# Gate blocks: the one-hot array of second indices stored token by token instead of four tokens interleaved

## The chip, the cores and the metric

One core of one Trainium2 chip. The metric is device microseconds of one execution of the whole program, taken as the median of several runs. Lower is better.

## What is computed

Two transformer-like blocks on 512 tokens of width 1024, all in float32 at the interface. What matters here is the second half of the first block, a mixture over 16384 tiny experts (128 x 128 keys), cut from the reference:

```python
sc = jnp.einsum('phcd,hcnd->phcn', q, sub_keys)            # 8 heads, 2 halves, 128 keys
top_s, top_i = lax.top_k(sc, 16)                           # best 16 keys of each half
cand_s = top_s[:, :, 0, :, None] + top_s[:, :, 1, None, :] # 16 x 16 pairs
best_s, best_pos = lax.top_k(cand_s, 16)
idx = take_along_axis(cand_i, best_pos)                    # i * 128 + j of 16 experts per head
g = softmax(best_s)
act = gelu(einsum('phkd,pd->phk', expert_u[idx], xb))
out = einsum('phk,phkd->pd', g * act, expert_v[idx])
```

So each token selects 128 experts (8 heads times 16), each with an index pair (i, j) and a weight g.

## The kernel before

The kernel runs the first block (`first`), the experts (`peer`) and the second block (`second`) one after the other. Float32 products are made of three passes: `split` writes a high part (ScalarE, L93) and a low part (L94) of an operand, and `mm3` issues three matmuls per 128-row piece (L116, L118, L119).

In `peer`, the first 384 tokens (three tiles of 128) don't gather their experts. They multiply by all 16384 of them, in 128 steps of 128 experts: a **u-step** (`u_step`) makes the activations of 128 experts for 384 tokens, with 24 matmuls of 384 columns into the tile `act`; a later v-step multiplies these by the gates and by `expert_v` (tile `po`). The gates are a table in DRAM, `gdram`, with g at [j, i] of each token and zeros elsewhere. The fourth tile of tokens gathers rows of its experts with indirect DMAs (`gsteps`, tile `row`), with the dot products on VectorE (L656).

**The gate table** is built in `gates(tt)` for one tile of 128 tokens, in 16 **blocks** of 8 tokens. After a transpose, partition = one of the token's 128 choices, column = token. Per block, VectorE writes three float16 arrays of 128 x 1024: `oj` is 1 where column j equals the choice's j (L807, `is_equal`), `oi` the same for i (L808), `oa` = `oi` times the high half of g (L809), and `oi` is overwritten with `oi` times the low half (L810). All three are laid out [2 groups][128 columns][4 tokens]: the four tokens of a group are interleaved, so the 128 columns of one token lie 4 elements (8 bytes) apart. Then `products` issues, per token, two matmuls that accumulate into one 128 x 128 piece of the tile `pg`: weights `oj` against moving `oa` (L820), and weights `oj` against moving `oi` (L822). Each matmul loads its weights anew. That makes 16 matmuls with 16 weight loads a block and 768 of each in the 48 blocks. ScalarE copies `pg` to the tile `stage` (L824, twice a block); every second block one DMA takes `stage` to `gdram`.

The arrays of a block come from a pool with 4 buffers (`ohp`), so VectorE can be four blocks ahead of TensorE. `pg` has 3 buffers, `stage` 2.

**What sets the order.** `chain()` is a generator that emits top-k work (`choose`), then the gates of tile order[1], the last `choose`, and the gates of order[2] and order[3]. Each `yield` reports an estimated VectorE cost. A planner adds these costs up in `now`, and TensorE's in `pe`: 4.2 a u-step and 1.8 a block's products. Whenever `pe` is behind `now`, it emits a u-step (which adds 1.25 to `now` if its low parts are made on VectorE, as in `gates`) and, after two of three of them, one step of the fourth tile's gathers (1.3). The products of a block are put off by 9 units of `now`. It holds back the last 10 of the 88 u-steps of this stage until the chain has ended. The order in which each engine then runs its work is made from this emission order by a scheduler at build time, which can move instructions past each other where data and buffers allow. After the stage, the angles of the second block are computed in a `stage` buffer (`tr`) and stored (`csd`), and the v-steps begin with a load of `gdram` (tile `G`).

The lines that are touched: L695 to L698 (the column numbers 0 to 127: `io32` as int32, `iota4` as float16, each number four times), L806 and L807 (`oj`), L820 and L822 (the weight operand), and L831 (the estimated VectorE cost of a block).

Of the kernel before, what the change touches and what calls it, by code (L numbers as in the profile page):

```python
# [7 lines left out]
F32 = mybir.dt.float32  # L8
F32R = mybir.dt.float32r
F16 = mybir.dt.float16  # L10
I32 = mybir.dt.int32
U32 = mybir.dt.uint32
AF = mybir.ActivationFunctionType
ALU = mybir.AluOpType
# [4 lines left out]
P = 128  # L19
# [50 lines left out]
class K:  # L70
# [516 lines left out]
    def peer(self):  # L587
# [3 lines left out]
        with ExitStack() as ctx:  # L591
# [99 lines left out]
            for r in range(16):  # L691
                nc.gpsimd.memset(stc[:, r], float(STARTS[r]))
                nc.gpsimd.memset(wtc[:, r], float(STARTS[r] - STARTS[r - 1]) if r else 0.0)
                nc.gpsimd.memset(btc[:, r], float(r))
            io32 = tkp.tile([P, P], I32, name="io32")  # L695
            nc.gpsimd.iota(io32, pattern=[[1, P]], base=0, channel_multiplier=0)
            iota4 = tkp.tile([P, P, 4], F16, name="iota4")
            nc.vector.tensor_copy(iota4, io32[:, :, None].to_broadcast([P, P, 4]))  # L698
            consts = (stc, wtc, btc)

# [39 lines left out]
            with ExitStack() as pctx:  # L740
                rp.append(self.pool("ring", 1, None, rctx, "right"))
                stgp = self.pool("stg", 2, ctx=pctx)
                ohp = self.pool("oh", 4, ctx=pctx)
                pps = self.pool("pps", 2, PSUM, pctx)
                pgs = self.pool("pgs", 3, PSUM, pctx)
                pacts.append(self.pool("pact2", 1, PSUM, pctx))


                now, pe = [0.0], [U_LATE]
                queue = []  # L750

                def later(fn, cost=0.0):
                    queue.append((now[0] + LAG, fn, cost))

                def drain(all=False):
                    while queue and (all or queue[0][0] <= now[0]):
                        _, fn, cost = queue.pop(0)
                        first = fn()
                        if cost:
                            self.after(first, u_mark[0])  # L760
                            pe[0] += cost

                def choose(n):
                    tt = order[n]
                    res = gres if tt == NT else {n: tkp.tile([P, P], F32, name="tr" + n, bufs=2) for n in "ijg"}

                    def load():
                        if n + 1 < len(order):
                            sc[0] = score_tile()
                            nc.sync.dma_start(sc[0].rearrange("p a b -> p (a b)"), scd[order[n + 1]])  # L770

                    yield from self.topk(sc[0], tkp, consts, res, load)
                    if tt == NT:
                        gf = tkp.tile([P, P], F32, name="gf")
                        nc.vector.scalar_tensor_tensor(gf, gres["i"], 128.0, gres["j"], op0=ALU.mult, op1=ALU.add)
                        nc.vector.tensor_copy(gidx, gf)
                        self.early = 0
                    else:
                        def turn():
                            pt = turned[tt] = pps.tile([P, 3, P], F32, name="pt", tag="pps")  # L780
                            return [nc.tensor.transpose(pt[:, n], res[x], self.ident) for n, x in enumerate("ijg")][0]

                        later(turn, 0.4)

                turned = {}

                def gates(tt):

                    while tt not in turned:
                        yield 0.5, False  # L790
                    pt = turned[tt]
                    it = tkp.tile([P, 2, P], F16, name="it", bufs=2)
                    nc.vector.tensor_copy(it, pt[:, :2])
                    gs = tkp.tile([P, P], F32, name="gs", bufs=2)
                    nc.vector.tensor_scalar(gs, pt[:, 2], 2048.0, None, op0=ALU.mult)
                    gt = tkp.tile([P, 2, P], F16, name="gt", bufs=2)
                    nc.vector.tensor_copy(gt[:, 0], gs)
                    nc.vector.tensor_tensor(gt[:, 1], gs, gt[:, 0], op=ALU.subtract)
                    yield 1.0, False
                    stage = {}  # L800
                    for n in range(P // 8):
                        def bc(x):
                            return x[:, n * 8:n * 8 + 8].rearrange("p (g t) -> p g t", t=4)[:, :, None, :] \
                                .to_broadcast([P, 2, P, 4])
                        io = iota4[:, None].to_broadcast([P, 2, P, 4])
                        oj, oi, oa = [ohp.tile([P, 2, P, 4], F16, name=x) for x in ("oj", "oi", "oa")]  # L806
                        nc.vector.tensor_tensor(oj, io, bc(it[:, 1]), op=ALU.is_equal)  # L807
                        nc.vector.tensor_tensor(oi, io, bc(it[:, 0]), op=ALU.is_equal)  # L808
                        nc.vector.tensor_tensor(oa, oi, bc(gt[:, 0]), op=ALU.mult)  # L809
                        nc.vector.tensor_tensor(oi, oi, bc(gt[:, 1]), op=ALU.mult)  # L810

                        def products(n=n, oj=oj, oi=oi, oa=oa):
                            b, half = divmod(n, 2)
                            if half == 0:
                                stage[b] = stgp.tile([P, P, TB], F32, name="stage", tag="stage")
                            first = None
                            for q in range(2):
                                ps = pgs.tile([P, 4, P], F32, name="pg")
                                for t in range(4):
                                    ins = nc.tensor.matmul(ps[:, t], oj[:, q, :, t], oa[:, q, :, t], start=True, stop=False)  # L820
                                    first = first or ins
                                    nc.tensor.matmul(ps[:, t], oj[:, q, :, t], oi[:, q, :, t], start=False, stop=True)  # L822
                                c = half * 8 + q * 4
                                nc.scalar.activation(stage[b][:, :, c:c + 4].rearrange("p i t -> p t i"), ps,  # L824
                                                     AF.Copy, scale=1.0 / 2048.0)
                            if half:
                                nc.sync.dma_start(gdram[tt * (P // TB) + b], stage[b])
                            return first

                        later(products, G_PE)  # L830
                        yield 2.8, False  # L831

                def chain():
                    for n in range(3):
                        yield from choose(n)
                    yield from gates(order[1])
                    yield from choose(3)
                    yield from gates(order[2])
                    yield from gates(order[3])

                todo = list(range(SP + RING))
                self.early = -1

                def row():
                    if 0 <= self.early < P:
                        next(gs)
                        self.early += 1
                        now[0] += ROW_DVE

                def u_next(single):  # L850
                    u_step(todo.pop(0), nc.gpsimd if single else nc.vector)
                    pe[0] += U_PE
                    if not single:
                        now[0] += LO_DVE

                for cost, single in chain():
                    now[0] += cost
                    drain()
                    while pe[0] < now[0] and len(todo) > U_TAIL:
                        u_next(single)  # L860
                        if len(todo) % 3:
                            row()
                while todo:
                    now[0] = max(now[0], pe[0])
                    drain()
                    u_next(False)
                    for _ in range(2):
                        row()
                drain(True)


                tr = stgp.tile([P, 4, T], F32, name="tr", tag="stage")
                posi = tr[:, 0].bitcast(I32)
                nc.sync.dma_start(posi, a["pos"].to_broadcast([P, T]))
                nc.vector.tensor_copy(tr[:, 1], posi)
                hpi = tkp.tile([P, 1], F32, name="hpi")
                nc.vector.memset(hpi, float(np.pi / 2))
                self.trig(tr[:, 2], tr[:, 1], tr[:, 3], hpi)
                nc.sync.dma_start(self.csd, tr[:, 2])
# [686 lines left out]
```

## Time and profile before

| | us |
|---|---|
| median of 3 runs | 2316.94 (2315.74 to 2318.61) |
| profiled execution | 2316.84 |
| its span, first to last instruction | 2315.1 |
| TensorE busy | 2191.9 |
| VectorE busy | 1654.0 |
| ScalarE busy | 924.1 |
| GpSimd busy | 529.9 |

The profile is of one execution. A row of a group gives the line, the engine, the operation, what it writes and reads, the count, the busy time in us and the mean in ns of one. PE is TensorE's matmuls, PEld its weight loads, DVE is VectorE, ACT ScalarE, POOL GpSimd. The ends of matmuls are modelled, so the pace of matmuls is read from the starts of successive rows.

### The profile page before, as it was taken

The page shows a single profiled execution, that of the slowest core. Times are in us where ns is not written, and L with a number is a line of the kernel's source. Part 1 is how long each engine was busy: PE and PEld are TensorE (multiplying, and loading weights), DVE is VectorE, ACT ScalarE, POOL GpSimd, SP SyncE. Part 2 cuts the span into 40 slices and gives each one's busy share as a digit, 9 for nine tenths or more (in the row PEclk, how much of TensorE's full clock was granted, in tenths as well). Part 3 has the DMA queues.
Part 4 walks back from the last instruction along what each step waited for, and adds up shares of the span by engine and source line. Part 5 has one row for each costly group of instructions (what it writes and reads, how often), then busy time and mean ns, then how long its engine had stood idle before and what let it go on. Part 6 is the DMA issues. An engine that isn't in the chain of part 4 may idle for free.

```text
span 2315.1 us, 29877 instructions
## 1 busy us (share of the span) xinstructions
PE 2191.9 (95%) x11063; PEld 1901.6 (82%) x11063; DVE 1654.0 (71%) x3118; ACT 924.1 (40%) x1346; POOL 529.9 (23%) x453
## 2 busy tenths in 40 slices
PE   4999997899999779999999999999999999999998
PEld 4888797799999658787998898878877878888887
DVE  8785699999778747767699887976666665444423
ACT  3623443245466423333333333354445554333321
POOL 3020033415112312223366553320122100000000
PEclk9989999999999889999999999999999999999999
DMA  7482356677777899889799898842221353223222
GB/s 279 141 292 80 128 209 221 214 262 278 259 257 261 288 303 315 298 307 316 270 363 372 311 343 300 291 168 83 83 74 57 113 179 112 91 92 108 75 88 74
DMA packets 158307, 483.66 MB, mean 209 GB/s; under 512 B 12232, under 2 KB 80456, under 8 KB 128080
## 3 DMA queue, kind: packets, MB, share of 16 engines
q1 hardware_dynamic: 116688, 330.73, 40.9%
q0 software_dynamic: 41472, 151.01, 18.6%
q8 instruction: 87, 1.43, 0.2%
q14 instruction: 60, 0.49, 0.1%
HBM read 429.65 MB, written 52.05 MB: 208 GB/s over the span
## 4 chain that ended last, share of the span: by engine, by line
PE 79%; DVE 10%; issue 6%; DMA 2%; POOL 2%; ACT 2%; DVEq 0%; POOLq 0%; ACTq 0%; SPq 0%
PE mm L116 12%; PE mm L118 12%; PE mm L119 12%; PE act L119 6%; PE act L116 6%; PE act L118 6%; PE po L118 5%; PE po L119 5%; PE po L116 5%; PE pg L820 2%; PE pg L822 2%; POOL row L642 2%; DVE row L656 1%; DVE ix L496 1%; DMA sp<-actd 1%
## 5 line engine op out<-in xcount | busy, mean ns | idle before, releaser
L93 ACT ACTIVATE whi<-raw 128x1024 fp32r<-128x1024 f32 (+1 forms) x415 | 428.9, 1036 | 499.0 <-PE act L118 216.0
L94 DVE TENSOR_TENSOR wlo<-raw,whi 128x1024 fp32r<-128x1024 f32 (+1 forms) x385 | 461.1, 1200 | 221.9 <-ACT whi L93 214.4
L118 PE MATMUL mm<-hl,whi 128*128 128x512 f32 x928 | 367.0, 396 | 4.2 <-DVE hl L972 2.1
L116 PE MATMUL mm<-hh,whi 128*128 128x512 f32 x928 | 366.1, 398 | 4.5 <-ACT hh L472 1.6
L119 PE MATMUL act<-hh,wlo 128*128 128x384 f32 x1024 | 348.4, 341 | 17.3 <-DVE wlo L94 13.3
L119 PE MATMUL mm<-hh,wlo 128*128 128x512 f32 x928 | 362.6, 396 | 0.0
L116 PE MATMUL act<-hh,whi 128*128 128x384 f32 x1024 | 349.5, 341 | 1.0 <-ACT sp L613 1.0
L118 PE MATMUL act<-hl,whi 128*128 128x384 f32 x1024 | 347.2, 339 | 0.0
L116 PE MATMUL po<-whi,ch 128*128 128x512 f32 x768 | 281.5, 393 | 33.9 <-ACT ch L93 32.4
L118 PE MATMUL po<-wlo,ch 128*128 128x512 f32 x768 | 302.4, 394 | 7.0 <-DVE wlo L94 7.0
L119 PE MATMUL po<-whi,cl 128*128 128x512 f32 x768 | 294.6, 391 | 0.0
L642 POOL DMA_INDIRECT row<-in_eu_dram,gidx x128 | 167.0, 1305 | 516.9 <-DVE row L656 430.2
L642 POOL DMA_INDIRECT row<-in_ev_dram,gidx x128 | 189.3, 1479 | 197.2 <-DVE acc L673 145.0
L118 PEld LDWEIGHTS mm<-hl,whi 128*128 128x128 f32 x928 | 176.7, 190 | 42.5 <-DVE hl L972 3.0
L116 PEld LDWEIGHTS mm<-hh,whi 128*128 128x128 f32 x928 | 176.4, 191 | 42.1 <-ACT hh L472 1.8
L119 PEld LDWEIGHTS act<-hh,wlo 128*128 128x128 f32 x1024 | 194.7, 190 | 19.5 <-DVE wlo L94 14.4
L119 PEld LDWEIGHTS mm<-hh,wlo 128*128 128x128 f32 x928 | 176.5, 190 | 36.9 <-DVE wlo L94 0.5
L116 PEld LDWEIGHTS act<-hh,whi 128*128 128x128 f32 x1024 | 195.1, 191 | 3.5 <-ACT sp L613 1.3
L116 PEld LDWEIGHTS po<-whi,ch 128*128 128x128 f32 x768 | 145.1, 189 | 64.1 <-ACT ch L93 32.7
L118 PEld LDWEIGHTS act<-hl,whi 128*128 128x128 f32 x1024 | 194.9, 190 | 1.6
L93 ACT ACTIVATE ch<-cf 128x384 fp32r<-128x384 f32 x128 | 67.1, 525 | 322.9 <-PE po L118 146.8
L118 PEld LDWEIGHTS po<-wlo,ch 128*128 128x128 f32 x768 | 145.4, 189 | 39.1 <-DVE wlo L94 9.5
(477 smaller groups left out, 3430.6 us busy)
## 6 DMA issues: line engine op xcount, KB each, us to landing
raw<-in_uT_dram SPq DMA_DIRECT2D x64, 1024.0 KB, 6.9
raw<-in_v_dram SPq DMA_DIRECT2D x64, 1024.0 KB, 7.8
raw<-in_w_in_dram SPq DMA_DIRECT2D x26, 1024.0 KB, 4.9
gdram<-stage SPq DMA_DIRECT2D x24, 1024.0 KB, 4.8
G<-gdram SPq DMA_DIRECT2D x16, 1536.0 KB, 12.9
raw<-in_w_gu_dram SPq DMA_DIRECT2D x22, 1024.0 KB, 4.9
actd<-sp SPq DMA_DIRECT2D x66, 192.0 KB, 3.8
sp<-actd SPq DMA_DIRECT2D x66, 192.0 KB, 5.1
```

The lines of the kernel that those rows point to most:

```text
L93: self.nc.scalar.activation(hi, src, AF.Copy)
L94: (eng or self.nc.vector).tensor_tensor(lo, src, hi.bitcast(F32), op=ALU.subtract)
L116: ins = nc.tensor.matmul(out, wh, xh, start=start and i == 0, stop=False)
L118: nc.tensor.matmul(out, wh, xl, start=False, stop=False)
L119: nc.tensor.matmul(out, wl, xh, start=False, stop=stop and i == n - 1)
L496: nc.vector.max_index(ix[:, hc, lo:lo + 8], s1[:, hc, lo:lo + 8], sc[:, hc])
L642: nc.gpsimd.indirect_dma_start(out=row, out_offset=None, in_=a[n], in_offset=bass.IndirectOffsetOnAxis(ap=gidx[:, k:k + 1], axis=0))
L656: ins = nc.vector.scalar_tensor_tensor(row, row, 1.0, self.h2g, op0=ALU.mult, op1=ALU.mult, accum_out=dots[:, n:n + 1])
L820: ins = nc.tensor.matmul(ps[:, t], oj[:, q, :, t], oa[:, q, :, t], start=True, stop=False)
L822: nc.tensor.matmul(ps[:, t], oj[:, q, :, t], oi[:, q, :, t], start=False, stop=True)
```

## The change

`oj` is laid out [8 tokens][128 columns]: the 128 columns of one token lie next to each other. VectorE writes it from a second table of column numbers, `iota1` (each number once), and an operand in which one token's index is repeated for 128 columns. The matmuls load `oj[:, token]`. `oi` and `oa`, the moving operands, stay interleaved. The estimated cost of a block in the planner goes from 2.8 to 3.2. `io32` moves into one of the two buffers of the tile `tri`, and one small copy makes `iota1`.

```diff
-            io32 = tkp.tile([P, P], I32, name="io32")
+            io32 = tkp.tile([P, P], F32, name="tri", bufs=2).bitcast(I32)
...
+            iota1 = tkp.tile([P, P], F16, name="iota1")
+            nc.vector.tensor_copy(iota1, io32)
...
-                        oj, oi, oa = [ohp.tile([P, 2, P, 4], F16, name=x) for x in ("oj", "oi", "oa")]
-                        nc.vector.tensor_tensor(oj, io, bc(it[:, 1]), op=ALU.is_equal)
+                        oj = ohp.tile([P, 8, P], F16, name="oj")
+                        oi, oa = [ohp.tile([P, 2, P, 4], F16, name=x) for x in ("oi", "oa")]
+                        nc.vector.tensor_tensor(oj, iota1[:, None].to_broadcast([P, 8, P]),
+                                                it[:, 1, n * 8:n * 8 + 8][:, :, None].to_broadcast([P, 8, P]),
+                                                op=ALU.is_equal)
...
-                                    ins = nc.tensor.matmul(ps[:, t], oj[:, q, :, t], oa[:, q, :, t], start=True, stop=False)
+                                    ins = nc.tensor.matmul(ps[:, t], oj[:, q * 4 + t], oa[:, q, :, t], start=True, stop=False)
                                     first = first or ins
-                                    nc.tensor.matmul(ps[:, t], oj[:, q, :, t], oi[:, q, :, t], start=False, stop=True)
+                                    nc.tensor.matmul(ps[:, t], oj[:, q * 4 + t], oi[:, q, :, t], start=False, stop=True)
...
-                        yield 2.8, False
+                        yield 3.2, False
```

## Rows read from the trace of the kernel before

**Rows 1.** Page, part 1: busy us, share of the span, instructions.

```profile
PE   2191.9 (95%) x11063; PEld 1901.6 (82%) x11063; DVE 1654.0 (71%) x3118; ACT 924.1 (40%) x1346; POOL 529.9 (23%) x453
```

**Rows 2.** Busy us (instructions) by stretch: length, PE, PEld, DVE, ACT, POOL, clock, DMA.

```profile
300.00:480.00 180.00, 154.99 (x865) 152.33 (x864) 179.90 (x752) 63.88 (x86) 69.48 (x40) 0.95 0.67 227
480.00:786.00 306.00, 306.00 (x1998) 292.81 (x1998) 256.48 (x445) 170.11 (x202) 75.96 (x50) 1.00 0.76 268
...
480.00:600.00 120.00, 120.00 (x771) 115.13 (x771) 117.31 (x239) 64.63 (x78) 42.67 (x22) 1.00 0.78 273
600.00:786.00 186.00, 186.00 (x1229) 177.68 (x1228) 139.18 (x207) 105.48 (x125) 33.29 (x28) 1.00 0.74 264
```

**Rows 3.** Groups by line and form, whole span: busy us, mean ns | idle before, releaser.

```profile
L824 ACT ACTIVATE stage<-pg 128x512 f32<-128x512 f32 x96 | 97.2, 1102 | 50.6 <-PE pg L822 39.3 <-issue 9.4 <-ACT ring L617 1.0
L820 PE MATMUL pg<-oa,oj 128*128 128x128 f16 x384 | 95.1, 296 | 0.0
L820 PEld LDWEIGHTS <-oj 128*128 128x128 f16 x384 | 44.5, 118 | 8.9 <-issue 7.6 <-DVE oj L807 0.2 <-DVE oa L809 0.2
L807 DVE TENSOR_TENSOR oj<-iota,it 128x1024 f16<-128x1024 f16 x48 | 36.9, 769 | 20.4 <-PE pg L822 20.2
```

**Rows 4.** Timeline of PE from 484.36 us: start, us, line, operation.

```profile
484.36 0.33 PE L118 MATMUL act<-hl,whi 128*128 128x384 f32 x1
484.54 0.28 PE L820 MATMUL pg<-oa,oj 128*128 128x128 f16 x1
484.64 0.30 PE L822 MATMUL pg<-oi,oj 128*128 128x128 f16 x1
484.76 0.30 PE L820 MATMUL pg<-oa,oj 128*128 128x128 f16 x1
```

**Rows 5.** Timeline of PEld in the same stretch: the weight loads.

```profile
484.18 0.19 PEld L118 LDWEIGHTS act<-hl,whi 128*128 128x128 f32 x1
484.54 0.11 PEld L820 LDWEIGHTS <-oj 128*128 128x128 f16 x1 [0.16 <-issue]
...
484.65 0.12 PEld L820 LDWEIGHTS <-oj 128*128 128x128 f16 x1
484.77 0.12 PEld L822 LDWEIGHTS <-oj 128*128 128x128 f16 x1
```

**Rows 6.** Timeline of PE in the second block's attention: matmuls of 128 float32 columns.

```profile
1626.23 0.22 PE L116 MATMUL o<-uph,uv 128*128 128x128 f32 x1
1626.29 0.28 PE L118 MATMUL o<-upl,uv 128*128 128x128 f32 x1
1626.40 0.28 PE L119 MATMUL o<-uph,uv 128*128 128x128 f32 x1
```

**Rows 7.** One line's instructions: a weight load of 8 columns, min/median/max in ns.

```profile
L1163 PEld LDWEIGHTS lf<-ident,uv x4: 83/84/86, 1601.2 to 1601.5; 128*8 128x8 f32 x4
```

**Rows 8.** Timeline of DVE: float32 and float16 operations of 1024 elements in succession.

```profile
466.21 0.68 DVE L808 TENSOR_TENSOR oi<-iota,it 128x1024 f16<-128x1024 f16 x1
466.81 0.68 DVE L807 TENSOR_TENSOR oj<-iota,it 128x1024 f16<-128x1024 f16 x1
467.41 0.68 DVE L808 TENSOR_TENSOR oi<-iota,it 128x1024 f16<-128x1024 f16 x1
...
469.49 1.20 DVE L656 SCALAR_TENSOR_TENSOR row<-row,h2g 128x1024 f32<-128x1024 f32 x1
470.62 0.08 DVE L656 DVE_READ_ACCUMULATOR row<-row,h2g 128x1 f32 x1
```

**Rows 9.** One line's instructions: the copy that makes the column numbers.

```profile
L698 DVE CAST iota<-io x1: 416/416/416, 258.3 to 258.3; 128x512 f16<-128x512 int32 x1
```

**Rows 10.** Chain that ended last, 785 to 850 us: what follows the stage.

```profile
811.14 6.08 DMA csd<-tr
817.31 8.00 DMA G<-gdram
...
826.50 0.79 PE po L116
```

## The prediction

> **What bounds the kernel now.** I began with the busy shares of the whole span: TensorE 95%, VectorE 71% [rows 1]. An average says little about one stage, so the next view is busy time by stretch. The gate blocks run from 480 to 786 us. There TensorE is busy for all of 306.00 us at a granted clock of 1.00 (2.4 GHz) [rows 2]. VectorE is busy 256.48 us of it, but unevenly: 117.31 of 120 us up to 600, 139.18 of 186 us after that; from 300 to 480 us it has no rest at all (179.90 of 180) [rows 2]. So TensorE sets the time of this stage, VectorE is full in its first part and has 46.8 us to spare in its second. When the stage ends, the angles are stored, G is loaded and only then do the v-steps start [rows 10]; nothing on that chain can start before the stage's last blocks, so a change of the stage's end goes to the end of the program one for one.
>
> What TensorE does in a block is read from starts. Matmuls of the gates follow each other at 484.64, 484.76 and so on: 0.118 us each [rows 4]. 48 blocks of 16 are 768 matmuls, 768 x 0.118 = 90.6 us of the 306. Their loads take 0.118 us in the mean [rows 3]; each is issued within 0.01 us of the start of the matmul in front (484.64 and 484.65, 484.76 and 484.77), and the next matmul starts as it ends (484.65 + 0.12 = 484.77) [rows 4, 5]. The first load of a block is not issued early either: it goes out at 484.54, 0.18 us after the float32 matmul in front of it started at 484.36, together with its own matmul [rows 4, 5]. Read so, the load is on the path, and the pace is the load's duration.
>
> **The change part by part.**
>
> Loads. The 768 loads stay; each reads 256 bytes in a row where it read 1024 bytes with gaps. Bounds of the pace: at the upper end nothing changes, 0.118 us. At the lower end a load that is fully hidden leaves the matmul's own pace: two matmuls of 128 columns start 0.06 us apart (1626.23, 1626.29) where the second's load was ready [rows 6]. I exclude that a load of packed columns gets slower, as it reads the same columns from a quarter of the space. Between the ends lies the row of a load of 8 columns, 0.084 us [rows 7]: that much a load takes almost without columns, so 0.034 of the 0.118 us belong to the 128 columns. That row is the nearest in kind, and would put the pace at 0.086; I take the middle of the two ends, 0.089 us, close to it. That saves 768 x 0.029 = 22.3 us of TensorE time, 16 blocks' worth (7.4 us) before 600 and 32 blocks' worth (14.8 us) after it.
>
> The Trainium skill has a figure for this: TensorE: Matmul & The Clock Gate, section Back-to-back issue gap, gives about 81 ns a matmul for a sustained stream of loads and matmuls of 128 columns. By it the sum would be 768 x 0.037 = 28 us; no run here shows that pace yet.
>
> VectorE, `oj`. The two-operand float16 operations of a block follow each other every 0.60 us (466.21, 466.81, 467.41), float32 ones of the same 1024 elements take 1.13 us (469.49 to 470.62) [rows 8]. All four float16 operations of a block run through at least four different elements at a stretch; the new `oj` has an operand that stands still for 128. No row shows that, so its price lies between 0.60 and 1.14 us. I take 1.14, the end that can undo the gain: two results at a time need two elements at a time from both operands. That adds 48 x 0.54 = 26 us to VectorE, and a block goes from 2.40 to 2.94 us. Below nothing is excluded, since no operation leaves. Where it falls: about 20 blocks' operations run before 600, where VectorE is full, so some 10 us of other work (the top-k of the fourth tile, wanted only by the third gate tile) moves past 600. After 600 VectorE then has 139 + 10 + 28 x 0.54 = 164 us of work, and TensorE 186 - 15 = 171. TensorE stays the bound, by 7 us.
>
> Planner. 3.2 for 2.8 emits more u-steps between blocks. Going through its loop with the constants in the code gives 10, 14, 10, 9 and 10 u-steps before (first gate tile, last top-k, second tile, third tile, held back), and 13, 14, 13, 3 and 10 after. So the third tile's 16 blocks have 3 u-steps among them. TensorE needs 16 x 16 x 0.089 = 22.8 us for these blocks, and 3 x 4.2 = 12.6 us for the u-steps (24 matmuls of 0.175 us: 306 - 90.6 us over the other 1230), 35 us in all; VectorE 16 x 2.94 + 6 x 1.15 = 54 us, less the four blocks that it can be ahead, 12 us: 42. TensorE waits some 6 us there unless held-back u-steps move up. I add 2 us for the first part, where VectorE is full and low parts of three more u-steps come in. Together 8 us are given back. The steps of the gathers are 69 in both, so nothing moves to the v-steps.
>
> ScalarE copies a block in 2 x 1.10 us [rows 3], under VectorE's 2.94; it stays hidden, and would cost 0.3 us a block if TensorE and VectorE were both quicker than that. `iota1` is one copy of a quarter of `iota4`'s 0.416 us at 258 us, beside other VectorE work [rows 9]: at most 0.4 us if not covered. `io32` takes one turn of the two `tri` buffers; its readers are done at 259 us, two top-ks before the buffer is used again, so no wait is added. The DMAs of the stage are the same in number and order.
>
> Sum: 2316.84 (the profiled execution, 1.7 us over its span and 0.1 under the median) - 22.3 + 8 = 2302.5; against the median **2303 us**.
>
> The range of this case alone: with the pace at 0.06 TensorE would save 44.5 us, but VectorE's 256 + 24 us of work in the stage caps the gain at 26, and 4 or more are given back: 2295. With the pace at 0.105 (10 us saved, 8 given back) 2315. So 2295 to 2315.
>
> **The rivals.**
>
> The load isn't what sets the pace. Then a packed `oj` does nothing for TensorE. For it: a float32 load of as many columns takes 0.19 us [rows 5] and yet matmuls of 128 columns behind it go every 0.11 us (1626.29, 1626.40) [rows 6], so a load record of 0.12 could hide; and a gate matmul lasts 0.296 us [rows 3] against 0.22 for one of 128 float32 columns [rows 6], as if the moving `oa`, still interleaved, were the slow side. Against it: loads end as matmuls start, row after row [rows 4, 5]. TensorE's 306 us stay, VectorE's 280 fit beneath: 2317, up to 2319. The Trainium skill speaks for this one (SBUF — State Buffer, section Door 1: The DMA port swizzle, the note on cachelines): two accesses to a 16-byte line are enough for full bandwidth, and a step of 8 bytes has two. By that rule the time stays at 2317.
>
> VectorE becomes the bound and the kernel gets slower. Place: the third gate tile, with 3 u-steps for 16 blocks. Without a quicker load TensorE has 16 x 1.89 + 12.6 = 43 us there, VectorE 54 us. With a full lead of four blocks nothing is lost, without any lead 11 us. It decides from the point at which VectorE's lead at the start of that tile is under three blocks; VectorE waited 20.2 us for TensorE's buffers before [rows 3], so the lead was there, but 26 us of new work would use it up. Time: 2321 to 2328.
>
> That `oj` stays at 0.60 us is possible too: then VectorE is out of the question, and with the forecast's loads 2297 would come out, inside the range.
>
> **How the numbers follow.** A measurement of this kernel can tell about 0.2% (4.6 us) from no change. The forecast (load on the path, pace between 0.06 and 0.105) gets 0.50, of which 0.03 lies within 0.2%; the load off the path with VectorE hidden 0.27; VectorE the bound 0.23. Faster 0.47, same 0.30, slower 0.23. The range for 8 in 10 runs from 2294 to 2323: below it 0.03 is left, above it more than half of the slow case.
>
> **What would show it.** Right: float16 loads under 0.10 us, starts of gate matmuls 0.08 to 0.10 apart, `oj` at 1.1 to 1.2 us, TensorE still nearly full in the blocks, the first matmul of the v-steps near 812 us instead of 826.50 [rows 10], the rest shifted by the same. Wrong: the pace still 0.118 with shorter loads (first rival); TensorE idle behind `oj` or `oi` in the last blocks (second); a gain in the stage that comes back in the wait for G. A reordering by the scheduler elsewhere, in the last top-k above all, could move a few us either way, and nothing in the rows prices that.

## The result and the profile after

The changed kernel takes 2338.84 us in the median (2334.90 to 2339.02), against 2317.03 us for the kernel before on the same chip: a ratio of 1.0082, with a 95% interval of 1.0070 to 1.0094. It is 0.8% slower. The profiled execution has a span of 2336.6 us, 21.5 us more than the 2315.1 us of before.

The busy shares, page part 1 of the kernel after, in the columns of [rows 1]:

```profile
PE 2196.9 (94%) x11063; PEld 1907.6 (82%) x11063; DVE 1681.9 (72%) x3118; ACT 922.0 (39%) x1346; POOL 532.8 (23%) x454
```

TensorE has no less to do than before (2196.9 us for 2191.9), and VectorE has 27.9 us more. The gate groups by line and form, in the columns of [rows 3] (L825 and L827 are the matmuls that were L820 and L822, L810 is `oj`):

```profile
L825 PE MATMUL pg<-oa,oj 128*128 128x128 f16 x384 | 92.8, 292 | 7.3 <-ACT stage L829 4.5 <-DVE oa L814 2.8
L827 PE MATMUL pg<-oi,oj 128*128 128x128 f16 x384 | 88.7, 294 | 5.2 <-DVE oi L815 5.2
L810 DVE TENSOR_TENSOR oj<-iota,it 128x1024 f16<-128x1024 f16 x48 | 65.6, 1366 | 15.0 <-PE pg L827 15.0
L827 PEld LDWEIGHTS <-oj 128*128 128x128 f16 x384 | 43.9, 114 | 7.1 <-issue 6.9
```

The load of packed columns takes 114 ns in the mean where the interleaved one took 118 [rows 3]. `oj` takes 1366 ns instead of 769 [rows 3]; that is 28.7 us over 48 blocks, as much as VectorE's whole growth. And the gate matmuls, which had no idle time ahead of them before [rows 3], now wait for `oa`, `oi` and `stage`. How far apart the matmuls start is read from the timeline of PE (start, us, line, operation):

```profile
700.72 0.30 PE L825 MATMUL pg<-oa,oj 128*128 128x128 f16 x1
700.84 0.29 PE L827 MATMUL pg<-oi,oj 128*128 128x128 f16 x1
700.95 0.30 PE L825 MATMUL pg<-oa,oj 128*128 128x128 f16 x1
701.07 0.30 PE L827 MATMUL pg<-oi,oj 128*128 128x128 f16 x1
```

In the median over the stage they start 0.116 us apart, against 0.118 before [rows 4]. The gain that the forecast rested on isn't there: 768 x 0.002 = 1.5 us.

Where the loss sits is read from busy time by stretch, in the columns of [rows 2] (length, PE, PEld, DVE, ACT, POOL, clock, DMA):

```profile
600.00:786.00 186.00, 184.47 (x1194) 178.74 (x1193) 156.43 (x215) 97.06 (x119) 39.00 (x32) 1.00 0.76 268
786.00:800.00 14.00, 7.41 (x62) 6.71 (x60) 14.00 (x21) 6.53 (x8) 6.87 (x5) 0.56 0.69 226
800.00:820.00 20.00, 5.99 (x48) 5.09 (x46) 3.90 (x8) 6.53 (x8) 6.22 (x5) 0.63 0.91 336
```

From 600 to 786 us TensorE is still nearly full, as before. But it does other work there. The timeline of PE before, the last gate matmul and the last matmul of a u-step:

```profile
785.47 0.29 PE L822 MATMUL pg<-oi,oj 128*128 128x128 f16 x1
...
793.78 0.34 PE L119 MATMUL act<-hh,wlo 128*128 128x384 f32 x1
```

And after, the last matmul of a u-step and the last gate matmul:

```profile
777.87 0.34 PE L119 MATMUL act<-hh,wlo 128*128 128x384 f32 x1
...
808.67 0.29 PE L827 MATMUL pg<-oi,oj 128*128 128x128 f16 x1
```

The last u-step ends at 778.2 us (794.1 before), while the last gate matmul starts at 808.7 (785.5 before). From 778 on the u-steps are used up and some ten blocks, 157 matmuls, are left with nothing beside them. In 786 to 800 VectorE is busy for 14.00 of 14.00 us and TensorE for 7.41, at a granted clock of 0.56, near the lower of its two levels (1.2 GHz). The timeline of DVE shows what fills VectorE, and that of PE (second fence; in brackets idle time and its releaser) what TensorE waits for:

```profile
787.37 1.22 DVE L810 TENSOR_TENSOR oj<-iota,it 128x1024 f16<-128x1024 f16 x1
788.51 0.68 DVE L813 TENSOR_TENSOR oi<-iota,it 128x1024 f16<-128x1024 f16 x1
789.11 1.29 DVE L814 TENSOR_TENSOR oa<-oi,gt 128x1024 f16<-128x1024 f16 x2
790.32 1.22 DVE L656 SCALAR_TENSOR_TENSOR row<-row,h2g 128x1024 f32<-128x1024 f32 x1
...
791.46 1.22 DVE L656 SCALAR_TENSOR_TENSOR row<-row,h2g 128x1024 f32<-128x1024 f32 x1
...
793.81 1.31 DVE L815 TENSOR_TENSOR oi<-oi,gt 128x1024 f16<-128x1024 f16 x2
```

```profile
789.85 0.40 PE L825 MATMUL pg<-oa,oj 128*128 128x128 f16 x2 [2.55 <-DVE oa L814]
...
794.57 0.28 PE L827 MATMUL pg<-oi,oj 128*128 128x128 f16 x1 [3.83 <-DVE oi L815]
...
807.88 0.28 PE L825 MATMUL pg<-oa,oj 128*128 128x128 f16 x1 [2.20 <-ACT stage L829]
```

Undisturbed, `oj` holds VectorE for 1.14 us (787.37 to 788.51), `oi` for 0.60 (788.51 to 789.11). The dot products of the gathered rows (L656) stand between the blocks' operations, and TensorE waits 2.55 and 3.83 us. VectorE is not the only releaser, though: it has written the last block's arrays at 803.4 us, and the wait of 2.20 us at 807.88 is for ScalarE's copies to `stage`, which themselves wait for a store of `stage` to `gdram` (799.39 in the next fence). Of the 11.1 us that TensorE waits between 778 and 809, 6.6 are for `oa` and `oi` and 4.5 for `stage`. The lower clock costs these matmuls nothing: at a granted clock of 0.50, the lower level (794.60 to 796.00), they start every 0.116 us (794.67, 794.79, 794.90), as at 1.00. What follows the last block is read from the chain that ended last, in order of time (start, us, what):

```profile
799.39 7.31 DMA gdram<-stage
806.80 3.62 ACT stage L829 x4
...
811.25 8.67 DMA tr<-in_pos_dram
...
832.47 2.00 DMA csd<-tr
834.65 7.55 DMA G<-gdram
...
843.46 0.80 PE po L116
```

The v-steps start at 843.46 us instead of 826.50 [rows 10], 17.0 us later. The other 4.5 of the 21.5 us come behind that point and are not traced to a cause: from the first to the last matmul of the v-steps alone it takes 698.5 to 711.3 us in the traces of this case. The angles of the second block stand in the chain above in full: their buffer `tr` is one of the two of `stage`, so their positions are loaded when the store of late blocks has freed it, at 811.25. Before, that load went out at 784.2 and the u-steps that were left covered part of what follows; after, nothing does.

### The profile page after: what moved, and what is told of

It reads as the page before. It is cut to its first block, busy times and chain, and to the rows that moved or that the text cites. A ratio compares the mean times of both kernels' runs of the same rounds, so it can differ in the third digit from the quotient of the medians.

```text
span 2336.6 us, 29882 instructions
## 1 busy us (share of the span) xinstructions
PE 2196.9 (94%) x11063; PEld 1907.6 (82%) x11063; DVE 1681.9 (72%) x3118; ACT 922.0 (39%) x1346; POOL 532.8 (23%) x454
## 4 chain that ended last, share of the span: by engine, by line
PE 78%; DVE 14%; issue 3%; DMA 3%; ACT 2%; POOL 1%; DVEq 0%; SPq 0%; ACTq 0%; POOLq 0%
PE mm L116 12%; PE mm L118 12%; PE mm L119 12%; PE po L118 6%; PE po L116 6%; PE po L119 6%; PE act L119 5%; PE act L116 5%; PE act L118 5%; DVE row L656 2%; PE pg L827 1%; PE pg L825 1%; DVE ix L496 1%; DVE oj L810 1%; DVE wlo L94 1%
## 5 line engine op out<-in xcount | busy, mean ns | idle before, releaser
L116 PE MATMUL po<-whi,ch 128*128 128x512 f32 x768 | 287.5, 394 | 40.6 <-ACT ch L93 36.1
L642 POOL DMA_INDIRECT row<-in_eu_dram,gidx x128 | 172.7, 1349 | 534.0 <-DVE row L656 448.5
```

The costliest lines, as they stand in the source:

```text
L116: ins = nc.tensor.matmul(out, wh, xh, start=start and i == 0, stop=False)
L642: nc.gpsimd.indirect_dma_start(out=row, out_offset=None, in_=a[n], in_offset=bass.IndirectOffsetOnAxis(ap=gidx[:, k:k + 1], axis=0))
```

## The experiments

Ratios are to the kernel before, run on the same chip beside each experiment (medians 2317.86 to 2319.71 us).

**The estimate and the write, one without the other.** The changed kernel with the old estimated cost:

```diff
-                        yield 3.2, False
+                        yield 2.8, False
```

> The changed kernel with the planner's old cost of a block, 2.8, in place of 3.2: packed oj and its dear write stay, the emission order of u-steps is that of before in the gate blocks (10, 14, 10, 9, 10 in place of 13, 14, 13, 3, 10). Theory V (VectorE's dearer oj alone makes the loss): the time stays near the changed kernel's, 2333 to 2342 us. Theory P (the planner's new figure, which uses up the u-steps before the last blocks, makes the loss): most of the 22 us goes, 2317 to 2323 us, and u-steps again run until the last blocks. If each has a part: between, 2324 to 2332 us.

Measured: 2339.86 us, 1.0095 (1.0067 to 1.0124). And the kernel before with the new estimate:

```diff
-                        yield 2.8, False
+                        yield 3.2, False
```

> The kernel before with 3.2 in place of 2.8 and nothing else: oj interleaved and cheap. Theory V: within 5 us of 2317. Theory P: 2328 to 2340 us, with the last gate blocks after the last u-step and TensorE waiting between them. Together with the run of the changed kernel at 2.8 this gives a two by two table; if the two parts add, the two excesses over 2317 sum to about 22 us.

Measured: 2323.78 us, 1.0026 (1.0011 to 1.0042). So the estimate alone costs about 6 us: its last gate matmul starts at 803.6 us, and 56 gate matmuls stand behind the last u-step in the trace (none before). With the new `oj` the estimate makes no difference that the intervals show, and the loss is there with the old one too (last gate matmul at 807.9, 104 behind the last u-step). The two don't add up: either is enough to leave gate blocks behind the last u-step.

**The same write, stored interleaved.** An attempt to keep the dear write and undo the packed load:

```diff
-                        oj = ohp.tile([P, 8, P], F16, name="oj")
...
-                        nc.vector.tensor_tensor(oj, iota1[:, None].to_broadcast([P, 8, P]),
+                        oj = ohp.tile([P, 2, P, 4], F16, name="oj")
...
+                        nc.vector.tensor_tensor(oj.rearrange("p g j t -> p g t j"),
+                                                iota1[:, None, None].to_broadcast([P, 2, 4, P]),
...
-                                    ins = nc.tensor.matmul(ps[:, t], oj[:, q * 4 + t], oa[:, q, :, t], start=True, stop=False)
+                                    ins = nc.tensor.matmul(ps[:, t], oj[:, q, :, t], oa[:, q, :, t], start=True, stop=False)
```

> The changed kernel, planner at 3.2, with the same VectorE operation (column numbers once, the index repeated for 128 columns) but its output stored with four tokens interleaved as before, so only the layout that TensorE loads is undone. Theory M (the interleaved moving operands oa and oi set the pace of the gate matmuls, the load hides): the time is that of the changed kernel within 4 us, 2335 to 2343, and the pace goes back from 0.116 to 0.118 us. If the packed load had brought something that the dear write ate: 10 us or more slower than the changed kernel, 2349 us and up. The operation itself may cost more than 1.37 us with a stride in its output.

Measured: 2377.67 us, 1.0244 (1.0216 to 1.0272). It doesn't separate the two as it was meant to, since the write got dearer still; the group of `oj` by line and form:

```profile
L810 DVE TENSOR_TENSOR oj<-iota,it 128x1024 f16<-128x1024 f16 x48 | 124.1, 2586 | 2.8 <-PE pg L829 2.8
```

2586 ns instead of 1366, with the same reading side: storing every fourth element costs as much again. It shows the direction (VectorE is 20.00 of 20 us busy in 800 to 820 and in 820 to 840, the last gate matmul starts at 846.7), not the size.

**A dear write without the packed load.** The kernel before with the comparison for `oj` issued twice in succession:

```diff
                         nc.vector.tensor_tensor(oj, io, bc(it[:, 1]), op=ALU.is_equal)
+                        nc.vector.tensor_tensor(oj, io, bc(it[:, 1]), op=ALU.is_equal)
```

> The kernel before, interleaved arrays and its estimated cost of 2.8, with the comparison that writes oj issued twice in succession, so that VectorE spends about 2 x 0.68 = 1.37 us on it, as much as the changed kernel's oj (1.37 us), and the loads stay as before. The result is the same values. If all of the loss comes from VectorE's longer write of oj, this must land where the changed kernel with the estimate of 2.8 landed: 2335 to 2342, ratio 1.007 to 1.011, last gate matmul at 804 to 810 us, pace 0.118. If the packed layout costs something of its own (an access of its loads or of its writes that disturbs others), this stays well below: 2320 to 2328, last gate matmul before 800. If the packed load gave back a real gain, this is slower than that kernel by as much: 2345 or more.

Measured: 2330.69 us (2330.02 to 2338.66), 1.0057 (1.0035 to 1.0079). The same with the estimate at 3.2:

> The same double write with the estimated cost of 3.2, as in the changed kernel; the built order of TensorE has the same 157 gate matmuls behind the last u-step. If VectorE's time and the order explain the changed kernel between them, this is within 4 us of it: 2335 to 2343, ratio 1.007 to 1.011. If the layout has a part, it is below 2330. If the double write alone did it through data races for buffers rather than through time, the waits would be for buffers of the pool (pg L822 as the releaser of oj) and not for oa and oi in the last blocks.

Measured: 2333.84 us, 1.0063 (1.0040 to 1.0085). This is the cleaner control. VectorE is busy for as long as in the changed kernel, and the same number of gate matmuls, 157, stands behind the last u-step; page part 1 and a stretch of its profile:

```profile
PE 2199.2 (94%) x11063; PEld 1907.7 (82%) x11063; DVE 1682.0 (72%) x3165; ACT 922.7 (40%) x1346; POOL 536.4 (23%) x454
```

```profile
786.00:800.00 14.00, 7.24 (x57) 6.21 (x55) 14.00 (x25) 6.95 (x8) 4.78 (x5) 0.63 0.68 211
```

DVE 1682.0 us to 1681.9, the start of the last u-step's last matmul 777.1 us to 777.9, that of the last gate matmul 807.5 to 808.7, that of the v-steps 841.7 to 843.5: the stage of the changed kernel within two microseconds, with the interleaved load at its 118 ns. The waits are of the same kind too: the gate matmuls wait 2.2 us for `oa`, 5.3 for `oi` and 2.5 for `stage`. So most of the loss comes from VectorE's time and the order, not from the packed array. The two runs came out 4 us and 1 us under what was expected. The intervals meet (1.0070 to 1.0094 and 1.0040 to 1.0085), so whether some 4 us belong to the layout itself stays open.

**The moving operand packed, the weights not.** The pace is the point here; `oa` and `oi` are stored token by token, `oj` as before:

```diff
-                        oj, oi, oa = [ohp.tile([P, 2, P, 4], F16, name=x) for x in ("oj", "oi", "oa")]
+                        oj = ohp.tile([P, 2, P, 4], F16, name="oj")
+                        oi, oa = [ohp.tile([P, 8, P], F16, name=x) for x in ("oi", "oa")]
...
-                                    ins = nc.tensor.matmul(ps[:, t], oj[:, q, :, t], oa[:, q, :, t], start=True, stop=False)
+                                    ins = nc.tensor.matmul(ps[:, t], oj[:, q, :, t], oa[:, q * 4 + t], start=True, stop=False)
```

> The kernel before with oa and oi, the moving operands, packed token by token (three dear VectorE operations a block) and oj left interleaved; planner at 2.8. Theory M: gate matmuls start 0.055 to 0.09 us apart and last about 0.22 to 0.25 us. Theory L (the load is on the path, packed or not, with its latency of about 0.115 us): they stay 0.115 to 0.12 us apart. The time itself: VectorE gets 3 x 0.63 x 48 = 90 us more to do, so 2360 to 2400 us by either.

Measured: 2357.07 us in one run, 3 us under the expected range. The time goes with three dear operations a block (`oi`, `oa`, `oi` at 1261, 1303 and 1274 ns in the mean). The pace is what it was made for; timeline of PE, and of PEld in the same stretch:

```profile
700.38 0.22 PE L827 MATMUL pg<-oa,oj 128*128 128x128 f16 x1
700.43 0.22 PE L829 MATMUL pg<-oi,oj 128*128 128x128 f16 x1
700.49 0.22 PE L827 MATMUL pg<-oa,oj 128*128 128x128 f16 x1
```

```profile
700.38 0.11 PEld L829 LDWEIGHTS <-oj 128*128 128x128 f16 x1
700.43 0.11 PEld L827 LDWEIGHTS <-oj 128*128 128x128 f16 x1
700.49 0.11 PEld L829 LDWEIGHTS <-oj 128*128 128x128 f16 x1
```

Matmuls 0.056 us apart, behind loads of interleaved columns that last 0.11 us each. The load that starts at 700.38 ends at 700.49, but its own matmul (L829) starts at 700.43, and the next load too: the records of two loads overlap. So a load of 0.11 us hides behind a pace of 0.056, and the moving operand set the pace of 0.118 all along.

**Two tokens interleaved instead of four, in all three arrays.** If the step of the moving operand counts, 4 bytes may do where 8 don't, and the operands that VectorE reads still have two different elements in succession:

```diff
-            iota4 = tkp.tile([P, P, 4], F16, name="iota4")
-            nc.vector.tensor_copy(iota4, io32[:, :, None].to_broadcast([P, P, 4]))
+            iota2 = tkp.tile([P, P, 2], F16, name="iota2")
+            nc.vector.tensor_copy(iota2, io32[:, :, None].to_broadcast([P, P, 2]))
...
-                        oj, oi, oa = [ohp.tile([P, 2, P, 4], F16, name=x) for x in ("oj", "oi", "oa")]
+                        oj, oi, oa = [ohp.tile([P, 4, P, 2], F16, name=x) for x in ("oj", "oi", "oa")]
```

> The kernel before (planner at 2.8, same order of work on every engine) with two tokens interleaved instead of four in all three arrays: the columns of a token lie 4 bytes apart, and VectorE still sees two different elements at a stretch. Theory M (the step of the moving operand sets the pace): gate matmuls start 0.056 to 0.08 us apart instead of 0.118. If VectorE keeps 0.60 us for each of its four operations, TensorE is relieved of up to 768 x 0.06 = 46 us in the gate stage, where VectorE then becomes the bound: 2285 to 2305 us. If VectorE's operations fall to 1.14 us: 108 us more of them, 2370 us and up. Rival: a step of 4 bytes is as slow as one of 8, pace 0.118, time 2315 to 2320 us.

Measured: 2290.67 us, 0.9877 (0.9850 to 0.9903): 1.2% faster than before. Groups by line and form, the timeline of PE, and the second stretch of the gate blocks:

```profile
L820 PE MATMUL pg<-oa,oj 128*128 128x128 f16 x384 | 54.1, 221 | 2.0 <-DVE oa L809 2.0
L820 PEld LDWEIGHTS <-oj 128*128 128x128 f16 x384 | 36.3, 98 | 16.4 <-issue 13.0 <-DVE oa L809 2.2 <-DVE oi L808 0.3
L807 DVE TENSOR_TENSOR oj<-iota,it 128x1024 f16<-128x1024 f16 x48 | 32.9, 685 | 3.3 <-PE pg L822 3.1
```

```profile
701.88 0.22 PE L822 MATMUL pg<-oi,oj 128*128 128x128 f16 x1
701.93 0.22 PE L820 MATMUL pg<-oa,oj 128*128 128x128 f16 x1
701.99 0.22 PE L822 MATMUL pg<-oi,oj 128*128 128x128 f16 x1
```

```profile
600.00:786.00 186.00, 165.91 (x1278) 158.09 (x1276) 156.97 (x238) 111.74 (x134) 46.65 (x39) 0.96 0.85 302
```

The busy time of the gate matmuls of L820 falls from 95.1 us [rows 3] to 54.1 (pace 0.057), `oj` stays at the price of the interleaved one (685 ns), and the last gate matmul starts at 757.3 us. That is the step the change was after, in the operand that matters.

The same with the planner told that a block's products are cheaper:

```diff
-G_PE = 1.8
+G_PE = 0.9
```

> The kernel with two tokens interleaved, and the planner told that a block costs TensorE 0.9 instead of 1.8. By the build order the u-steps are then used up earlier and 160 gate matmuls stand behind the last u-step (8 in the kernel with 1.8). Theory O (gate blocks without u-steps among them run at VectorE's pace and cost time): slower than the kernel with 1.8 by 5 to 15 us. Rival: with a quick pace the order no longer matters, within 4 us of it.

Measured: 2303.49 us, 0.9944 (0.9922 to 0.9966), worse than without it. The estimate that is nearer to the measured 16 x 0.057 us emits u-steps earlier; the last one ends at 744.4 us, 160 gate matmuls are left behind it, and the last of these starts at 772.1. Here too, u-steps that run out before the blocks cost more than the estimate corrects.

**The order held.** The changed kernel, in which each of the last ten u-steps is made to follow one of the last ten blocks' products on TensorE:

```diff
+                blocks = []
...
-                        later(products, G_PE)
+                        def marked(products=products):
+                            blocks.append(products())
+                            return blocks[-1]
+
+                        later(marked, G_PE)
...
+                    self.after(u_mark[0], blocks[min(38 + U_TAIL - len(todo) - 1, len(blocks) - 1)])
```

> The changed kernel with one thing more: each of the last ten u-steps is pinned behind one of the last ten gate blocks, so that in TensorE's order 15 gate matmuls stand behind the last u-step instead of 157. All the costs are the changed kernel's (packed oj, 1.37 us on VectorE, planner at 3.2). Theory O (the loss comes from the order: u-steps run ahead and the last blocks then wait for VectorE uncovered): 2320 to 2328 us. Theory T (VectorE's total is simply too large for the stage): 2334 to 2342 us, whatever the order.

Measured: 2324.10 us, 1.0025 (1.0013 to 1.0038). Of 0.82% only 0.25% is left, with the same `oj` (1368 ns). A stretch:

```profile
786.00:800.00 14.00, 14.00 (x92) 13.36 (x90) 11.52 (x18) 5.88 (x9) 5.04 (x5) 1.00 0.93 321
```

TensorE is full in 786 to 800 at a clock of 1.00. Its last gate matmul starts no earlier (807.5), but the work behind it now overlaps the last blocks: the positions are loaded at 803.4 us, and the v-steps start at 834.6 instead of 843.5.

**VectorE relieved.** The changed kernel, in which every second u-step of the last ones has its low part made by GpSimd:

```diff
-                    u_step(todo.pop(0), nc.gpsimd if single else nc.vector)
+                    e = todo.pop(0)
+                    single = single or (e >= 45 and e % 2 == 0)
+                    u_step(e, nc.gpsimd if single else nc.vector)
```

> The changed kernel with the low parts of every second u-step from the 46th on made by GpSimd instead of VectorE: some 17 x 1.2 = 20 us off VectorE's account, about what the dearer oj adds in the stage, and GpSimd takes about 3.7 us for each. By the build order 24 gate matmuls stand behind the last u-step. Theory O and theory T both expect most of the loss back, 2318 to 2328 us; if neither, that is if the loss sits in the packed layout or in the transition to the v-steps, it stays at 2333 to 2342 us.

Measured: 2340.42 us, 1.0088 (1.0064 to 1.0112), a miss. The stage itself does recover: the last gate matmul starts at 780.7 us and TensorE waits 0.7 and 1.6 us for `oa` and `oi`. But the time is given back behind it, as the chain shows:

```profile
809.39 5.09 DMA row<-in_eu_dram,gidx
...
825.10 19.38 DMA G<-gdram
```

GpSimd also issues the gathers, and with the low parts in its queue these go out late: the 66th is issued at 818.5 us instead of 779.4, the one in the chain lands at 814.5, and others are issued up to 832. The load of `G`, beside them, takes 19.38 us where it took 8.00 [rows 10], and the v-steps start at 845.7.

**The chain behind the last block shortened.** The changed kernel with the block of lines that computes the angles put ahead of all gate blocks:

```diff
+                tr = stgp.tile([P, 4, T], F32, name="tr", tag="stage")
+                posi = tr[:, 0].bitcast(I32)
+                nc.sync.dma_start(posi, a["pos"].to_broadcast([P, T]))
...
+                nc.sync.dma_start(self.csd, tr[:, 2])
                 ohp = self.pool("oh", 4, ctx=pctx)
```

> The changed kernel with the angles of the second block (load of the positions, trig, store) computed ahead of all gate blocks instead of behind the last one; everything else as it was, 157 gate matmuls behind the last u-step in the built order. In the changed kernel the positions are loaded at 811.25 us, when the buffer of the last block is free, and G is loaded only when the angles have been stored, 834.65. If the time behind the last gate block counts one for one, G is loaded once the last block is in DRAM, at 816 to 820, and the v-steps start at 825 to 829 instead of 843.5: 15 to 18 us less, of which VectorE's 9 to 10 us of trig come back if it is full where they land: 2320 to 2331 (ratio 1.001 to 1.006). If the v-steps are held by something else, the time stays at 2335 to 2342.

Measured: 2323.57 us, 1.0018 (1.0005 to 1.0030): some 15 us of the loss are back with the blocks as late as ever (last gate matmul at 814.3 us, 5.6 later, since VectorE was full where the angles went). The v-steps start at 834.0, later than the 825 to 829 expected: the last copy to `stage` ends at 816.0, the DMA queue then waits 8.3 us for its store, and the load of `G` goes out at 824.9 and is used from 832.9. The profiled execution (2317.75 us) is the quickest of ten, so its rows give more of the loss back than the median does. And the same on top of the two interleaved tokens:

> The kernel with two tokens interleaved in all three arrays, with the angles ahead of the gate blocks. There the v-steps started at 801.9 us, 44.6 us after the last gate matmul, with the angles stored at 786.2 and G's load behind them. If that chain is what counts, G is loaded when the last u-steps run and the v-steps start 15 to 25 us earlier, less 9 us that VectorE, full in this stage, takes for the angles: 2272 to 2286. If the gathers of the fourth tile hold the end of the stage instead, 2286 to 2293.

Measured: 2272.39 us, 0.9807 (0.9788 to 0.9826), the fastest of all: 1.9% under the kernel before. The v-steps start at 784.2 us.

## Why the prediction was wrong

**The load on the path: wrong, and the step on which the sign rested.** It was read from loads that end as the next matmul starts [rows 4, 5]. That was a coincidence: the pace set by the moving operand and the length of a load's record were both 0.118 us. Loads of 0.11 us behind matmuls that start every 0.056 us show that an end of a load's record releases nothing here, and that two loads' records can overlap. The first rival's mechanism is the right one, and the row that was weighed too lightly was the length of the matmul itself: 0.296 us for a gate matmul [rows 3] against 0.22 for one of 128 float32 columns [rows 6]. With packed or two-token moving operands it measures 0.22. In place of 22.3 us saved, 1.5 were.

The Trainium skill was cited for this rival (SBUF — State Buffer, section Door 1: The DMA port swizzle, the note on cachelines: two accesses to a 16-byte line are enough). For the load the runs don't contradict it, as packing it left the pace where it was. For the moving operand they do: 128 float16 columns 8 bytes apart are passed every 0.118 us, and every 0.057 or 0.056 when they are 4 or 2 bytes apart.

The Trainium skill's other sentence (TensorE: Matmul & The Clock Gate, section Back-to-back issue gap: about 81 ns for loads and matmuls of 128 columns) doesn't fit either side: 118 ns with the 8-byte step, 57 and 56 ns without it.

**The price of `oj`: right.** 1.14 us were taken, and VectorE's 26 us more; undisturbed it takes 1.14, its records are 1.37 long in the mean, and VectorE grew by 27.9 us.

**Hidden under TensorE, 6 + 2 us given back: wrong.** The forecast compared sums over the third tile and the stretch from 600 to 786 and found TensorE the bound by 7 us. TensorE was in fact full from 600 to 778 us. The step that failed is that its work would stay mixed to the end. The u-steps don't wait for VectorE's blocks and stand ahead of them in the order that was built; the blocks, each with a longer `oj` to wait for, collected at the end. There TensorE has nothing else, and 157 matmuls of 0.116 us (18.2 us) took from 778 to 809. The planner's estimate (3 u-steps in the third tile) pulls the same way, and alone cost 6 us. That this is the 6 that were put down is luck: the forecast's 6 contained the dear write, and beside the dear write the estimate made no difference.

**The second rival: right in kind, too small.** VectorE as the bound in the last blocks was priced at up to 11 us, 2321 to 2328. The stage ended 23 us later (785.5 to 808.7). The rival counted waits inside the third tile, with 3 u-steps among its blocks and 54 us of VectorE's work. In the trace VectorE takes from 704.4 to 803.4 us for that tile, because 14 low parts and 21 dot products of the gathers stand between its blocks' operations where 6 operations were counted; some nine u-steps run among its first blocks and none among its last. The rival also left out the wait for `stage`, and that whatever comes after the last block loses its cover when the u-steps are used up. The forecast did say that a change of the stage's end goes to the end of the program one for one, since nothing on the chain behind it could start earlier. Before, the positions' load did start earlier (784.2 us, with the last gate matmul at 785.5). Of 23.2 us 17.0 reached the start of the v-steps, as the work behind the last block took 34.8 us for 41.0.

**What the parts are worth.** With the order held, the loss falls from 0.82% to 0.25%; with the angles out of the chain, to 0.18%. No run has both, and as both shorten what stands uncovered behind the blocks they are not to be added. What is shown: a longer write of `oj`, without any packing, brings 0.63% in the same order; the packed load brings no gain that can be seen. Not settled: the 0.2% between that control and the changed kernel, which the intervals don't exclude as nothing.

**The signs named for the outcome.** Loads under 0.10 us: no, 0.114. Starts 0.08 to 0.10 apart: no, 0.116. `oj` at 1.1 to 1.2: yes, where nothing disturbs it. The v-steps near 812: no, 843.5. TensorE idle behind `oj` or `oi` in the last blocks: yes, behind `oa` and `oi`, the sign of the second rival; the pace that stayed is that of the first. Both rivals were true together, while each had been given its own time.

## What to carry to other kernels

A load that ends when the next matmul starts doesn't prove that the matmul waited for it: look for a place where the same load stands behind a quicker matmul, or change the strides of the moving operand and of the weights one at a time. When work is added to an engine that feeds the last part of a stage, ask what the other engine will have left to do by then, and not only whether its sum is larger: independent work can run ahead and leave the dependent part uncovered at the end. Layouts between the extremes are worth a run: two interleaved tokens gave TensorE nearly the packed pace (0.057 for 0.056 us), and VectorE's operations still followed each other every 0.60 us.

## What the runs showed of the hardware

- A float16 matmul of 128 columns, each with its own weight load, is issued every 0.056 us when the moving columns are 2 bytes apart, every 0.057 at 4 bytes and every 0.118 at 8 bytes. The columns of the weights at 8 bytes made no such difference: 0.056 with them, 0.116 for packed weights under an 8-byte moving operand.
- That pace didn't follow the granted clock with the 8-byte step: the matmuls started every 0.116 us at 1.00 and at 0.50 alike.
- The recorded length of a weight load is not its price. In the mean it was 118 ns interleaved by four under a pace of 0.118, 114 packed under 0.116, 122 interleaved by four under 0.056 and 98 interleaved by two under 0.057; under the quick paces the records of successive loads overlap.
- VectorE's two-operand float16 operations of 1024 elements followed each other every 0.60 us, whether the repeated operand alternates among four elements or between two. With one operand that stands still for 128 it was 1.14 us (records of 1366 ns in the mean), and with the result stored at every fourth element besides, records of 2586 ns.
- The load of `G` took 7.55 us after and 8.00 before, and 19.38 us when late gathers were in flight with it.
